# Inverse roots of all normalisations as one power on GpSimd, in a two-sequence encoder layer

## The chip, the cores and the metric

One NeuronCore of a Trainium2 chip. The core's engines are TensorE (PE; its weight loads are the rows "PEld"), VectorE (DVE), ScalarE (ACT), GpSimd (POOL), and SyncE (SP), which issues most DMAs. Each engine runs its own instructions in order and waits for the others through semaphores. The metric is the device time of one launch in microseconds; it covers both sequences and all weights.

## The reference

One encoder layer, run on two independent sequences of 512 tokens (`x_prompt`, `x_sample`), all in float32, with D = 1024 and a feed-forward width of 2816:

```python
def rms_norm(x, g):
    y = x * lax.rsqrt(jnp.mean(x * x, axis=-1, keepdims=True) + EPS)      # EPS = 1e-6
    return y * g

def encoder_layer(x, ...):
    x = x + 0.5 * swiglu(rms_norm(x, ffn1_norm), ffn1_w_gate, ffn1_w_up, ffn1_w_down)
    h = rms_norm(x, mix_norm)
    proj = h @ w_in                                  # 13 parts: aq ak av mq mk mv gates o g_att g_mlstm
    aq = apply_rope(rms_norm(aq, q_norm), cos, sin)  # 8 heads of 64, a root for each token and head
    ak = apply_rope(rms_norm(ak, k_norm), cos, sin)  # 2 heads of 64
    att = gqa_block_attention(aq, ak, av)
    mem = mlstm_bidirectional(mq, mk, mv, ...)       # 4 heads of 128, each head normalised by its rms
    merged = sigmoid(g_att) * (att @ w_up_att) + sigmoid(g_mlstm) * (mem @ w_up_mlstm)
    x = x + merged @ w_out
    x = x + 0.5 * swiglu(rms_norm(x, ffn2_norm), ffn2_w_gate, ffn2_w_up, ffn2_w_down)
    return x                                         # then rms_norm(x, final_norm)
```

Each `rms_norm` needs one number for each token (or token and head): 1/sqrt(mean of squares + EPS). How that number is made is what the change is about.

## The kernel before

**Layout and stages.** The residual stream of a sequence is kept transposed (`xs[s]`: channels on partitions, 8 blocks of 128, tokens along the row). For both sequences in turn there is a first feed-forward block, the mixing block (projections, attention, the mLSTM memory, merging, output projection), and a second feed-forward block; most products are made of high and low parts of the operands (`split`, `put`), each product several matmuls of 128x512. The weights of the first pass are split once, parked in DRAM and read again for the second sequence (`load_w`). Times in the profile by stage: first feed-forward of both sequences to about 655 us; mixing of the first sequence (s=0) to about 1015; mixing of the second (s=1) to about 1440; second feed-forward of both to 2060; final norm to the end.

**Order.** The program is written once, in Python, and a scheduler orders each engine's instructions by priority, which follows the order of writing; `with shifted(n)` moves what stands inside it later by n steps (or earlier, for n below 0). A shift is counted in written instructions, so an edit that removes some of them also moves others. On the chip each engine then keeps its order strictly: a matmul that waits for a small result holds up every matmul behind it.

**From squares to the root.** `sq_add` makes squares on ScalarE (L152, L155) and adds them on GpSimd (L156). `col_sums` turns the sums with TensorE (L203) into a PSUM bank and sums the rows on VectorE (L205): one column of sums for each block of 128 tokens, so 128x4 for a sequence. `rstd_cols` (L162) scales by 1/n and adds EPS, and `rsqrt_cols` makes the root on VectorE: a shift and a subtraction on the integer bits as first guess (L171, L173), then three Newton steps of three instructions each:

```python
        for _ in range(3):
            t = t_()
            V.scalar_tensor_tensor(t, y, -0.5, y, op0=ALU.mult, op1=ALU.mult)
            V.tensor_tensor(t, t, a, op=ALU.mult)
            r = t_()
            V.scalar_tensor_tensor(r, t, 1.5, y, op0=ALU.add, op1=ALU.mult)
            y = r
```

(L189, L190, L192.) With the scaling that is twelve instructions; without it, eleven. For a width of two the steps are written column by column (L177, L182, L184), fifteen instructions. `bcast_psum` turns the four columns with TensorE so that each token's root stands in every partition (L213), and `bcast_cols` copies that to SBUF (L219).

**Where roots are made.** There are 21 of them:

- two at the start, from token rows (`rows_rstd`, 128x4, sums L1258);
- one for each sequence ahead of the mixing block (`stats`, 128x4), near 655 and 760 us;
- one for the keys (`kv_done`, 128x8) and one for the queries (`q_done`, 128x32) of each sequence, near 674 and 697 us and near 1019 and 1041 us; their sums come from `sumsq` (L785). `rope_apply` multiplies by the root (L796) and rotates; `q_rope` turns the rotated queries with TensorE (L941);
- four for the memory's heads of each sequence (128x4), from 861 to 948 and from 1250 to 1331 us; the broadcast is written 160 steps later (`shifted(160)`);
- one for each sequence ahead of the second feed-forward block (128x4), near 1154 and 1441 us;
- one for the final norm of the first sequence (`finish0`, 128x4), near 2062 us, and two for the second (`finish1`, two columns each, for the token blocks 0, 1 and 2, 3).

**The last microseconds.** `finish1_upper` turns and squares the upper channels of the second sequence; `finish1(th)` turns the lower ones (L1411), squares them in two parts (`square`, L1437), adds the sums (L1457, L1460), makes the root, and `put_out` multiplies (L1418 on VectorE, L1420 on ScalarE, L1422 on VectorE) and stores (L1423). L606 is VectorE's eviction of the last down projection, which adds the residual.

GpSimd does little besides the additions L156: copies of gates (L868), a gate of the memory's output, a table (L699), and the issue of a few small DMAs (the gains of the norms, among others).

Of the kernel before, what the change touches and what calls it, by code (L numbers as in the profile page):

```python
# [8 lines left out]
F32 = mybir.dt.float32  # L9
F32R = mybir.dt.float32r  # L10
I32 = mybir.dt.int32
AF = mybir.ActivationFunctionType
ALU = mybir.AluOpType
# [3 lines left out]
P = 128  # L17
S = 512
D = 1024
# [3 lines left out]
EPS = 1e-6  # L23
# [3 lines left out]
def encoder(ctx, tc, I, outs):  # L27
    nc = tc.nc
    cpool = ctx.enter_context(tc.tile_pool(name="cpool", bufs=1))
# [4 lines left out]
    spool = ctx.enter_context(tc.tile_pool(name="spool", bufs=4))  # L34
# [7 lines left out]
    def nm(s):  # L42
        n_id[0] += 1
        return f"{s}_{n_id[0]}"
# [71 lines left out]
    def PT():  # L116
        return pt.tile([P, S], F32, tag="t", name=nm("pst"))
# [9 lines left out]
    make_identity(nc, ident)  # L127
    ones = cpool.tile([P, P], F32, name="ones")
    nc.vector.memset(ones, 1.0)
    pw = PT()[:, 0:P]  # L130
    warm = cpool.tile([P, 1], F32, name="warm")
    nc.scalar.activation(warm, ones[:, 0:1], AF.Silu)
# [16 lines left out]
    def sq_add(src, acc, tag="t2", qtag="f2", eng=None):  # L149
        if acc is None:  # L150
            acc = T2(F32, tag)
            nc.scalar.activation(acc, src, AF.Square)  # L152
            return acc
        q = T2(F32, qtag)
        nc.scalar.activation(q, src, AF.Square)  # L155
        (eng or nc.gpsimd).tensor_tensor(acc, acc, q, op=ALU.add)  # L156
        return acc

    def rstd_cols(v, width, n):

        a = spool.tile([P, width], F32, tag=f"rs{width}", bufs=5 if width > 2 else 10, name=nm("rs"))
        nc.vector.tensor_scalar(a, v, 1.0 / n, EPS, op0=ALU.mult, op1=ALU.add)  # L162
        return rsqrt_cols(a, width)

    def rsqrt_cols(a, width):

        def t_(dt=F32):
            return spool.tile([P, width], dt, tag=f"rs{width}", bufs=5 if width > 2 else 10, name=nm("rs"))
        V = nc.vector
        b = t_(I32)  # L170
        V.tensor_scalar(b, a.bitcast(I32), 1, None, op0=ALU.logical_shift_right)  # L171
        y_ = t_(I32)
        V.tensor_scalar(y_, b, -1.0, 1597463007.0, op0=ALU.mult, op1=ALU.add)  # L173
        y = y_.bitcast(F32)
        if width <= 2:
            h = spool.tile([P, width], F32, tag=f"rsh{width}", bufs=2, name=nm("rsh"))
            V.tensor_scalar(h, a, -0.5, None, op0=ALU.mult)  # L177
            cols = [slice(i, i + 1) for i in range(width)]
            for _ in range(3):
                t, r = t_(), t_()  # L180
                for c in cols:
                    V.scalar_tensor_tensor(t[:, c], y[:, c], h[:, c], y[:, c], op0=ALU.mult, op1=ALU.mult)  # L182
                for c in cols:
                    V.scalar_tensor_tensor(r[:, c], t[:, c], 1.5, y[:, c], op0=ALU.add, op1=ALU.mult)  # L184
                y = r
            return y
        for _ in range(3):
            t = t_()
            V.scalar_tensor_tensor(t, y, -0.5, y, op0=ALU.mult, op1=ALU.mult)  # L189
            V.tensor_tensor(t, t, a, op=ALU.mult)  # L190
            r = t_()
            V.scalar_tensor_tensor(r, t, 1.5, y, op0=ALU.add, op1=ALU.mult)  # L192
            y = r
        return y

    def stats(acc):

        return rstd_cols(col_sums(acc), 4, D)

    def col_sums(acc, bs=(0, 1, 2, 3)):  # L200
        p = PT()
# [558 lines left out]
    def mix(s, xh, xl, early=None, extra=None, after=None):  # L760
# [20 lines left out]

        def sumsq(t, to):
            q2 = T2()
            nc.scalar.activation(q2, t, AF.Square)
            V_.tensor_reduce(to, q2.rearrange("p (h e) -> p h e", e=DA), axis=AX.X, op=ALU.add)  # L785

        def rope_apply(t, rq, tab, bsel):
# [25 lines left out]
        def kv_done(pk):  # L813
            for b in range(4):
                nc.scalar.activation(kraw3[:, b, :], pk[b][:, 0:P], AF.Copy, scale=r[s][:, b:b + 1])
                nc.scalar.activation(Gt[:, b * 16:(b + 1) * 16], pk[b][:, 2 * P:2 * P + 16], AF.Copy,
                                     scale=r[s][:, b:b + 1])
                pv = pk[b][:, P:2 * P].rearrange("p (k e) -> p k e", k=HK)
                nc.scalar.activation(Vst[:, b, :, 0:DA], pv, AF.Copy, scale=r[s][:, b:b + 1])
                V_.scalar_tensor_tensor(Vst[:, b, :, DA:2 * DA], pv, r[s][:, b:b + 1], f(Vst[:, b, :, 0:DA]),  # L820
                                        op0=ALU.mult, op1=ALU.subtract)
            ssk = small(8, "ssk")
            sumsq(kraw, ssk)
            ko = rope_apply(kraw, rstd_cols(ssk, 8, DA), tabs[1], None)
            ko3 = ko.rearrange("p (g e) -> p g e", e=DA)
            nc.scalar.activation(kst[:, :, 0, 0, :], ko3, AF.Copy)
            nc.scalar.activation(kst[:, :, 0, 1, :], ko3, AF.Copy)
            V_.tensor_tensor(kst[:, :, 1, 0, :], ko3, f(kst[:, :, 0, 0, :]), op=ALU.subtract)
            V_.tensor_tensor(kst[:, :, 1, 1, :], ko3, f(kst[:, :, 0, 1, :]), op=ALU.subtract)
# [3 lines left out]
        def q_done(pq):  # L833
            ssq = small(32, "ssq")
            for b in range(4):
                t = T2()
                nc.scalar.activation(t, pq[b], AF.Copy, scale=r[s][:, b:b + 1])
                sumsq(t, ssq[:, b * 8:(b + 1) * 8])
                qraw.append(t)
            rq.append(rstd_cols(ssq, 32, DA))  # L840

        def k_turn():
            for hk in range(HK):
# [306 lines left out]
        def mem_out(h, Ts):  # L1150
            vm = Vm[0]
            po = PO()
            hs_ = slice(h * P, (h + 1) * P)
            turned = []
            for j in range(4 + 1):
                if j < 4:
                    p = PT()
                    for i in range(4):
                        nc.tensor.transpose(p[:, i * P:(i + 1) * P], Ts[i][0][:, j * P:(j + 1) * P], ident)
                    ph, pl = T2(F32R), T2(F32R)  # L1160
                    split(p, ph, pl)
                    turned.append((j, ph, pl))
                if j >= 1:
                    t, ph, pl = turned.pop(0)
                    with shifted(15):
                        for n, (a, b) in enumerate(((0, ph), (1, ph), (0, pl))):
                            nc.tensor.matmul(po, vm[:, a, t, hs_], b, start=(t == 0 and n == 0),  # L1167
                                             stop=(t == 3 and n == 2))
            h2 = T2()
            nc.scalar.activation(h2, po, AF.Square)  # L1170
            og = ogs[h]
            V_.tensor_tensor(og, og, po, op=ALU.mult)
            rh = rstd_cols(col_sums(h2), 4, DM)
            with shifted(160):
                Rh = bcast_psum(rh)
                V_.tensor_tensor(og, og, Rh, op=ALU.mult)
                split(og, mem[:, h, 0, :], mem[:, h, 1, :])
# [70 lines left out]
    def rows_rstd(s, engines):  # L1248

        sq = [spool.tile([P, 4], F32, tag="cs4", bufs=4, name=nm("cs4")) for _ in range(2)]  # L1250
        for b in range(4):
            for i in range(2):
                x_, to = raws[s][:, b, i * S:(i + 1) * S], sq[i][:, b:b + 1]
                if engines[i] is V_:
                    V_.scalar_tensor_tensor(orow[3 + i], x_, 1.0, x_, op0=ALU.mult, op1=ALU.mult, accum_out=to)
                else:
                    nc.scalar.activation(orow[3 + i], x_, AF.Square, accum_out=to)
        V_.tensor_tensor(sq[0], sq[0], sq[1], op=ALU.add)  # L1258
        return rstd_cols(sq[0], 4, D)

    def scaled(to, x_, k, R_):
        V_.scalar_tensor_tensor(to, x_, g1[:, k:k + 1], R_, op0=ALU.mult, op1=ALU.mult)
# [184 lines left out]
    def finish1(th):  # L1447
        bs = slice(2 * th, 2 * th + 2)
        cut = 2 * P
        ps_ = PS(), PT()  # L1450
        for ks in (0, 1), (2, 3):
            for i in range(2):
                turn_out(1, 2 * th + i, 0, ps_[i], ks)
                if ks[0] == 0:
                    square(1, 2 * th + i, ps_[i][:, 0:cut])
        sm, a = small(2, "fs2"), small(2, "fs2")
        V_.scalar_tensor_tensor(sm, sq1[:, 0, bs], EPS, sq1[:, 1, bs], op0=ALU.add, op1=ALU.add)  # L1457
        for i in range(2):
            square(2, 2 * th + i, ps_[i][:, cut:S])
        V_.tensor_tensor(a, sm, sq1[:, 2, bs], op=ALU.add)  # L1460
        r = rsqrt_cols(a, 2)
        with shifted(0 if th else LATER):
            for j in range(4):
                i, half = j % 2, 1 - j // 2
                b = 2 * th + i
                put_out(1, b, half, upper[b] if half else ps_[i], r[:, i:i + 1])
# [55 lines left out]
```

## Time and profile before

| | us |
|---|---|
| median of 3 runs | 2086.05 (2085.86 to 2088.21) |
| the profiled execution | 2088.21 |
| its span in the profile | 2088.2 |
| TensorE busy | 2063.1 (99%), 9488 matmuls |
| VectorE busy | 1573.0 (75%), 2870 instructions |
| ScalarE busy | 894.6 (43%), 1645 instructions |
| GpSimd busy | 100.3 (5%), 106 instructions |

Busy time counts from a record's start to its end, and matmuls are pipelined, so a busy TensorE need not be one at its peak. The granted TensorE clock is at nine tenths or more of full speed in all 40 slices of the span. In rows of the timeline the first number is the start in us from the beginning of the span, the second the length in us; then engine, line, operation, output<-inputs with shape, and a count; a bracket at the end gives the engine's idle time before it and what ended it. In rows of groups (by line) stand busy time in us, the mean of one in ns, and the idle time just before them. "L171" is line 171 of the kernel.

### The profile page before, as it was taken

What the parts mean: (1) busy time and instruction counts of PE and PEld (TensorE: products, weight loads), DVE (VectorE), ACT (ScalarE), POOL (GpSimd) and SP (SyncE); (2) the same over time, 40 slices, a digit from 0 to 9 for tenths busy, and PEclk for the clock granted to TensorE, in tenths of its full rate; (3) what the DMA queues carried; (4) which work ended last, traced back from release to release, by engine and by line L of the source; (5) the groups of instructions that cost most, each with busy time, mean ns of one, the idle gap of its engine ahead of it and who ended that gap; (6) DMA issues with size and microseconds to landing.
All of it is one profiled execution on the core that took longest, in us unless ns stands there. A gap on an engine that the chain in (4) does not pass through costs nothing.

```text
span 2088.2 us, 27312 instructions
## 1 busy us (share of the span) xinstructions
PE 2063.1 (99%) x9488; PEld 1694.4 (81%) x9488; DVE 1573.0 (75%) x2870; ACT 894.6 (43%) x1645; POOL 100.3 (5%) x106
## 2 busy tenths in 40 slices
PE   8999999999999999999999999999999999999998
PEld 6888888888888877888877788888888888888887
DVE  6888888786797899575557945545888888785797
ACT  6544444443234566463344543324444444442222
POOL 1000000001003012000110000001000000000010
PEclk9999999999999999999999999999999999999999
DMA  8656555699766655777675345677656555599753
GB/s 274 203 174 197 192 171 182 204 343 358 260 225 245 213 170 198 259 234 272 204 273 191 121 152 185 206 247 248 203 170 213 186 177 182 182 350 343 272 189 115
DMA packets 304186, 458.53 MB, mean 220 GB/s; under 512 B 20304, under 2 KB 170848, under 8 KB 303024
## 3 DMA queue, kind: packets, MB, share of 16 engines
q1 hardware_dynamic: 303456, 455.52, 64.9%
q0 software_dynamic: 592, 1.27, 0.3%
q8 instruction: 75, 1.23, 0.2%
q14 instruction: 63, 0.52, 0.1%
HBM read 289.82 MB, written 166.89 MB: 219 GB/s over the span
## 4 chain that ended last, share of the span: by engine, by line
PE 90%; DVE 4%; DMA 3%; ACT 1%; issue 1%; SPq 0%; DVEq 0%; POOL 0%; ACTq 0%; POOLq 0%
PE mm L755 18%; PE pss L333 17%; PE pst L333 11%; PE mm L333 9%; PE mm L589 9%; PE pst L589 4%; PE pss L589 4%; PE mm L739 4%; PE pso L589 3%; PE pso L739 1%; PE pso L1028 1%; PE pso L1167 1%; PE pss L1001 1%; PE pst L755 1%; PE pss L755 1%; PE pss L1117 1%
## 5 line engine op out<-in xcount | busy, mean ns | idle before, releaser
L755 PE MATMUL mm<-xh,w 128*128 128x512 f32 x896 | 292.2, 396 | 2.0 <-DMA w<-wpark 2.0
L333 PE MATMUL pss<-xc,w 128*128 128x512 f32 x1056 | 256.2, 391 | 1.0 <-DVE t L364 1.0
L333 PE MATMUL mm<-xc,w 128*128 128x512 f32 x1056 | 253.6, 391 | 3.3 <-ACT w L291 1.0
L333 PE MATMUL pst<-xc,w 128*128 128x512 f32 x1056 | 253.6, 389 | 0.0
L333 PEld LDWEIGHTS pss<-xc,w 128*128 128x128 f32 x1056 | 196.8, 188 | 48.3 <-DVE t L364 7.9
L333 PEld LDWEIGHTS mm<-xc,w 128*128 128x128 f32 x1056 | 197.2, 188 | 46.7 <-ACT w L291 2.0
L333 PEld LDWEIGHTS pst<-xc,w 128*128 128x128 f32 x1056 | 198.2, 188 | 41.2
L755 PEld LDWEIGHTS mm<-xh,w 128*128 128x128 f32 x896 | 168.0, 189 | 36.4 <-DVE f L1204 1.9
L589 PE MATMUL mm<-rt,w 128*128 128x512 f32 (+1 forms) x819 | 188.4, 384 | 0.0
L755 PE MATMUL mm<-xl,w 128*128 128x512 f32 x448 | 176.4, 394 | 0.0
L589 PEld LDWEIGHTS mm<-rt,w 128*128 128x128 f32 x819 | 151.3, 188 | 29.8
L291 ACT ACTIVATE w<-t 128x512 fp32r<-128x512 f32 x176 | 107.1, 627 | 141.1 <-issue 55.2
L292 DVE TENSOR_TENSOR w<-t,w 128x512 fp32r<-128x512 f32 x176 | 118.2, 687 | 51.8 <-ACT w L291 49.7
L333 PE MATMUL pss<-xc,f 128*128 128x512 f32 x528 | 126.8, 389 | 0.0
L333 PEld LDWEIGHTS pss<-xc,f 128*128 128x128 f32 x528 | 99.1, 188 | 20.6
L657 ACT ACTIVATE w<-wr 128x512 fp32r<-128x512 f32 x72 | 45.2, 632 | 138.1 <-PE pso L589 65.7
L755 PEld LDWEIGHTS mm<-xl,w 128*128 128x128 f32 x448 | 84.7, 189 | 17.0
L657 ACT ACTIVATE w<-t 128x512 fp32r<-128x512 f32 x82 | 51.8, 632 | 107.4 <-PE pst L589 62.4
L589 PE MATMUL pss<-rt,w 128*128 128x512 f32 x396 | 93.7, 389 | 0.0
L589 PE MATMUL pst<-rt,w 128*128 128x512 f32 x396 | 93.7, 389 | 0.0
L240 DVE TENSOR_TENSOR w<-wr,w 128x1024 fp32r<-128x1024 f32 (+1 forms) x56 | 69.6, 1243 | 23.6 <-ACT w L239 22.9
L589 PEld LDWEIGHTS pst<-rt,w 128*128 128x128 f32 x396 | 74.3, 188 | 15.4
(336 smaller groups left out, 3656.4 us busy)
## 6 DMA issues: line engine op xcount, KB each, us to landing
rt<-rbuf SPq DMA_DIRECT2D x154, 512.0 KB, 5.4
wpark<-w SPq DMA_DIRECT2D x104, 512.0 KB, 3.5
w<-wpark SPq DMA_DIRECT2D x104, 512.0 KB, 4.6
wr<-in_ffn_w_gate_dram SPq DMA_DIRECT2D x62, 512.0 KB, 5.2
rbuf<-tab SPq DMA_DIRECT2D x102, 256.0 KB, 4.0
wr<-in_ffn_w_up_dram SPq DMA_DIRECT2D x44, 512.0 KB, 4.6
rbuf<-f SPq DMA_DIRECT2D x72, 256.0 KB, 4.0
wr<-in_w_in_dram SPq DMA_DIRECT2D x36, 512.0 KB, 5.7
```

The lines of the kernel that those rows point to most:

```text
L240: pin(lo_eng.tensor_tensor(lo, raw, f(hi), op=ALU.subtract))
L291: pin(nc.scalar.activation(t[:, 0], src, AF.Copy))
L292: pin(V_.tensor_tensor(t[:, 1], src, f(t[:, 0]), op=ALU.subtract))
L333: nc.tensor.matmul(p, a[:, k, :], xt[:, b, k, :], start=(first and k == 0 and i == 0), stop=(k == HK_ - 1 and i == 2), skip_group_check=True)
L589: nc.tensor.matmul(p, u[:, a, d * P:(d + 1) * P], r[:, b, ts], start=(first and q == 0 and k == 0), stop=(q == len(us) - 1 and k == 2), sk ...
L657: nc.scalar.activation(hi, src, AF.Copy)
L739: nc.tensor.matmul(p[b][:, :N], a[:, k, bs], w_[:, kl, :], start=(k == 0 and i == 0), stop=(k == KD - 1 and i == 2))
L755: nc.tensor.matmul(p, a[:, k, :], b, start=(k == 0 and i == 0), stop=(k == n - 1 and i == 2))
L1001: nc.tensor.matmul(p, qT[:, h, b * P:(b + 1) * P], kv[:, hk * 2 + j, :], start=(j == 0), stop=(j == 1))
L1028: nc.tensor.matmul(po, Vst[:, kv_, hk, :], w, start=(kv_ == 0 and i == 0), stop=(kv_ == 3 and i == 1))
L1117: nc.tensor.matmul(p, qk[a][:, isl], qk[b], start=(n == 0), stop=(n == 2))
L1167: nc.tensor.matmul(po, vm[:, a, t, hs_], b, start=(t == 0 and n == 0), stop=(t == 3 and n == 2))
```

## The change

`rsqrt_cols` is gone. `rstd_cols` now takes sums of squares that carry 1/n already, adds EPS with one instruction of GpSimd (left out where the sums hold EPS already), and raises to the power -0.5 with a second one, whose exponents come from a constant tile `nhalf`. The squares get the factor n^-0.5 on ScalarE (`scale=`), where the kernel squares with ScalarE; at the start, where VectorE squares half of the rows, the factor 1/n stands in that instruction, and EPS is added where the two halves are summed. In all 21 powers and 17 additions of GpSimd take the place of 248 instructions of VectorE; the tiles of the small columns get 4 buffers instead of 5 or 10. What reads the roots, and how they are broadcast, is as before. The scheduler orders the whole program anew.

```diff
@@
+    nhalf = cpool.tile([P, 32], F32, name="nhalf")
+    nc.gpsimd.memset(nhalf, -0.5)
...
@@ sq_add
-            nc.scalar.activation(acc, src, AF.Square)
+            nc.scalar.activation(acc, src, AF.Square, scale=D ** -0.5)
...
-        nc.scalar.activation(q, src, AF.Square)
+        nc.scalar.activation(q, src, AF.Square, scale=D ** -0.5)
...
-    def rstd_cols(v, width, n):
-
-        a = spool.tile([P, width], F32, tag=f"rs{width}", bufs=5 if width > 2 else 10, name=nm("rs"))
-        nc.vector.tensor_scalar(a, v, 1.0 / n, EPS, op0=ALU.mult, op1=ALU.add)
-        return rsqrt_cols(a, width)
-
-    def rsqrt_cols(a, width):
...
+    def rstd_cols(v, width, eps=EPS):
+
+        a = spool.tile([P, width], F32, tag=f"rs{width}", bufs=4, name=nm("rs"))
+        if eps:
+            nc.gpsimd.tensor_scalar(a, v, eps, None, op0=ALU.add)
+            v = a
+        nc.gpsimd.tensor_tensor(a, v, nhalf[:, 0:width], op=ALU.pow)
+        return a
 
     def stats(acc):
 
-        return rstd_cols(col_sums(acc), 4, D)
+        return rstd_cols(col_sums(acc), 4)
...
@@ sumsq
-            nc.scalar.activation(q2, t, AF.Square)
+            nc.scalar.activation(q2, t, AF.Square, scale=DA ** -0.5)
...
@@ kv_done
-            ko = rope_apply(kraw, rstd_cols(ssk, 8, DA), tabs[1], None)
+            ko = rope_apply(kraw, rstd_cols(ssk, 8), tabs[1], None)
...
@@ q_done
-            rq.append(rstd_cols(ssq, 32, DA))
+            rq.append(rstd_cols(ssq, 32))
...
@@ mem_out
-            nc.scalar.activation(h2, po, AF.Square)
+            nc.scalar.activation(h2, po, AF.Square, scale=DM ** -0.5)
...
-            rh = rstd_cols(col_sums(h2), 4, DM)
+            rh = rstd_cols(col_sums(h2), 4)
...
@@ rows_rstd
-                    V_.scalar_tensor_tensor(orow[3 + i], x_, 1.0, x_, op0=ALU.mult, op1=ALU.mult, accum_out=to)
+                    V_.scalar_tensor_tensor(orow[3 + i], x_, 1.0 / D, x_, op0=ALU.mult, op1=ALU.mult, accum_out=to)
                 else:
-                    nc.scalar.activation(orow[3 + i], x_, AF.Square, accum_out=to)
-        V_.tensor_tensor(sq[0], sq[0], sq[1], op=ALU.add)
-        return rstd_cols(sq[0], 4, D)
+                    nc.scalar.activation(orow[3 + i], x_, AF.Square, scale=D ** -0.5, accum_out=to)
+        V_.scalar_tensor_tensor(sq[0], sq[0], EPS, sq[1], op0=ALU.add, op1=ALU.add)
+        return rstd_cols(sq[0], 4, 0)
...
@@ finish1
-        r = rsqrt_cols(a, 2)
+        r = rstd_cols(a, 2, 0)
```

More of the change, by code (lines that the diff above doesn't have):

```diff
@@ L165, in rsqrt_cols @@
-    def rsqrt_cols(a, width):
[L167 to L194, printed above, removed]
```

## The prediction

> **What bounds the kernel now.** I read the page first (busy shares), then the timeline at each place where an inverse root stands. From the page:
>
> ```profile
> span 2088.2 us, 27312 instructions
> ## 1 busy us (share of the span) xinstructions
> PE 2063.1 (99%) x9488; PEld 1694.4 (81%) x9488; DVE 1573.0 (75%) x2870; ACT 894.6 (43%) x1645; POOL 100.3 (5%) x106
> ```
>
> TensorE is the bound: 2063.1 of 2088.2 us. No saving elsewhere can reach the time except through its 25.1 us of idle time, and much of that lies at the two ends, before the first inputs have landed and after the last matmul. The change frees VectorE, which is busy for 75%. So the question is narrow: at which of the 21 inverse roots does TensorE wait, or the end depend, on the small VectorE instructions, and what stands there afterwards.
>
> **The prices.** GpSimd (POOL) executes no power now. Its nearest rows, by shape, and a handover from VectorE:
>
> ```profile
> L156 POOL TENSOR_TENSOR R<-R,f 128x512 f32<-128x512 f32 x17 | 24.8, 1460 | 156.1 <-ACT f L155 142.8 <-ACT R L152 12.7
> ...
> L699 POOL TENSOR_TENSOR tab<-f,gb 128x128 f32<-128x128 f32 x4 | 2.0, 521 | 0.0
> ```
>
> ```profile
> 672.17 0.23 DVE L862 TENSOR_TENSOR gt<-gt,gbias 128x64 f32<-128x64 f32 x1
> ...
> 672.46 0.20 POOL L868 COPY Fs<-gt 128x16 f32<-128x16 f32 x1 [1.41 <-DVE gt L862]
> ```
>
> A two-input pass costs (1460-521)/384 = 2.45 ns a column and 521-128x2.45 = 207 ns beside it. The eps addition on 4 columns is then 0.22 us. A handover costs 672.46-672.40 = 0.06, and I take the same for one out of POOL and between two of its own. With X for the power: from sums to root 0.06+0.22+0.06+X+0.06 = 0.4+X with the addition, 0.1+X without.
>
> X is the unknown. From below: one pass, 0.21 us for 4 columns and 0.28 for 32. From above, by rows: POOL does what the twelve VectorE instructions did, each at the price of a pass of its own, 12x0.21 = 2.5 us for 4 columns and 12x0.28 = 3.4 for 32. I take 0.2 us + 50 ns a column, an estimate: one dispatch, and in each column some twenty passes' worth of arithmetic, about twice the chain's operations, since a general power must handle any exponent. X is then 0.3 (2 columns), 0.4 (4), 1.8 (32): near the lower end, because the fixed price is paid once and not twelve times.
>
> **The end of the kernel: gain 1.75 us.** ScalarE there, and the last sums on VectorE:
>
> ```profile
> 2078.43 0.72 ACT L1420 ACTIVATE t<-t,rs 128x512 f32<-128x512 f32 x1
> 2079.04 0.38 ACT L1437 ACTIVATE f<-pss 128x256 f32<-128x256 f32 x1
> ...
> 2081.87 1.33 ACT L1420 ACTIVATE t<-t,rs 128x512 f32<-128x512 f32 x2 [2.00 <-DVE rs L184]
> ```
>
> ```profile
> 2079.91 0.16 DVE L1460 TENSOR_TENSOR fs<-fs,sq 128x2 f32<-128x2 f32 x1
> ```
>
> The last root is on the path: its sums are done at 2080.07, ScalarE starts on it at 2081.87, and the stores follow. These 1.80 us become 0.1+X = 0.4: 1.4 less. The first half's root moves too: in the new order its L1420 (at 2078.43 now) goes ahead of ScalarE's squares, so the square L1437 no longer queues behind it from 2078.43 to 2079.04. It can start when TensorE has turned its input; of the 0.61 us I take 0.35, and the last sums come that much earlier. Together 2.05-X = 1.75. The change adds a wait here: in VectorE's queue two evictions (L606), which TensorE's last transposes need, now stand behind an instruction that waits for the first root. That bites only where the power takes longer than the chain it replaces, some 2.4 us.
>
> **The query norms of the first sequence (128x32): loss 0.75 us.**
>
> ```profile
> 696.48 0.66 DVE L785 TENSOR_REDUCE ssq<-t 128x8 f32<-128x512 f32 x1
> ...
> 700.33 0.69 DVE L796 TENSOR_TENSOR t<-t,rs 128x512 f32<-128x512 f32 x1
> ...
> 704.30 1.04 PE L941 MATMUL pst<-ident,t 128*128 128x128 f32 x8
> ```
>
> The new program's order puts the first turning of rotated queries (L941) 1.8 us earlier, counted in the matmuls ahead of it: TensorE, strictly in order, arrives at 702.5. Its input takes 704.30-700.33, about 4.0 us, from the start of L796, which needs the root. The sums are done at 696.48+0.66 = 697.14 and the root at 697.55+X, so the turning can start at 701.55+X, and TensorE waits X-1.05 = 0.75. The same norm of the second sequence is done long before VectorE gets to its first use and costs nothing.
>
> **Broadcasts (L213) that come earlier in TensorE's order: loss 2.45 us before relief.** The column sums (L203, then VectorE's L205) at three of them:
>
> ```profile
> 756.75 0.63 PE L203 MATMUL pst<-ident,R 128*128 128x128 f32 x4
> ...
> 758.35 0.68 DVE L205 TENSOR_REDUCE cs<-pst 128x4 f32<-128x512 f32 x1
> ```
>
> ```profile
> 1150.66 0.60 PE L203 MATMUL pst<-ident,R 128*128 128x128 f32 x4
> ...
> 1151.65 0.68 DVE L205 TENSOR_REDUCE cs<-pst 128x4 f32<-128x512 f32 x1
> ```
>
> ```profile
> 1440.31 0.69 DVE L205 TENSOR_REDUCE cs<-pst 128x4 f32<-128x512 f32 x1 [0.75 <-PE pst L203]
> ...
> 1443.45 0.65 PE L213 MATMUL pst<-ident,rs 128*128 128x128 f32 x4 [0.18 <-DVE rs L192]
> ```
>
> Near 757 the broadcast followed L203 after 10.7 us of matmuls; in the new order after 2.5, and L203 itself stands 1.1 earlier: due at 756.75-1.1+2.5 = 758.15. Its sums are done at 759.03, the root at 759.43+X = 759.8: a wait of 1.65. Near 1151 the 10.3 us have become 1.8, due at 1152.46; sums 1152.33, root 1152.73+X = 1153.1: a wait of 0.65. Near 1441 it is due 1.8 earlier than the 1443.27 at which TensorE arrives now, 1441.47; root 1441.0+0.4+X = 1441.8: a wait of 0.35 against 0.18, loss 0.15. Of the other column roots the nearest to its use is a head's:
>
> ```profile
> 925.64 0.68 DVE L205 TENSOR_REDUCE cs<-pst 128x4 f32<-128x512 f32 x1
> ...
> 934.40 0.62 PE L213 MATMUL pst<-ident,rs 128*128 128x128 f32 x4
> ```
>
> It is due 6.2 us earlier, at 928.2, and stands at 926.32+0.4+X = 927.1, in time up to X = 1.5.
>
> **What is freed: gain 0.9.** In the first sequence's attention VectorE is nearly as full as TensorE (columns: length, then PE, PEld, DVE, ACT, POOL):
>
> ```profile
> 700.00:725.00 25.00, 25.00 (x130) 20.65 (x129) 24.30 (x50) 14.93 (x31) 0.00 (x0) 1.00 0.53 176
> 750.00:775.00 25.00, 24.16 (x124) 19.38 (x123) 23.72 (x54) 14.56 (x30) 4.69 (x4) 1.00 0.60 189
> 800.00:830.00 30.00, 29.16 (x140) 22.88 (x139) 25.50 (x58) 20.31 (x45) 6.70 (x4) 1.00 0.55 187
> ```
>
> In the second and the third row TensorE idles 0.84 us each beside a busy VectorE, some 1.8 us with the crumbs between. The query norms' chain and that of the 757 root leave VectorE there. I take half of the 1.8. Bounds: nothing; or all of it, and the 1.65 us wait too, if VectorE gets to the sums as soon as L203 allows.
>
> **The start: nothing.**
>
> ```profile
> 10.88 0.16 DVE L1258 TENSOR_TENSOR cs<-cs,cs 128x4 f32<-128x4 f32 x1
> ...
> 14.41 0.72 PEld L213 LDWEIGHTS pst<-ident,rs 128*128 128x128 f32 x4 [0.47 <-ACT t L1243]
> ...
> 36.04 1.06 ACT L291 ACTIVATE w<-wr 128x1024 fp32r<-128x1024 f32 x1 [1.05 <-DMA wr<-in_ffn_w_gate_dram]
> ```
>
> The first broadcast waits for a ScalarE copy (L1243) that frees its bank, 3.4 us after the sums: that covers the root until X passes 3.2. Four small gain loads on POOL's queue now stand behind the first two roots and go out near 30 us; nobody reads them before the first down projection ends. In SP's order one weight load moves ahead of a store: up to 1.05 gained at ScalarE's wait at 36.04, or lost, if the gain loads now collide with it. I take 0. Squares with a scale cost what squares without did, and the scaled sum replaces a plain one: nothing.
>
> **Sum.** -1.75 +0.75 +1.65 +0.65 +0.15 -0.9 = +0.55 us. With c the price of a column in us, X = 0.2+c x columns, it is -1.7+46c; 32 of the 46 are the query norms. The profiled execution took 2088.21 us with its span of 2088.2; the median of the three runs is 2.16 below. On the median: 2086.6 us.
>
> One more thing can lengthen POOL's instructions, its port:
>
> ```profile
> 659.32 9.00 POOL L156 TENSOR_TENSOR R<-R,f 128x512 f32<-128x512 f32 x5 [12.74 <-ACT R L152]
> ```
>
> Five additions took 9.00 where five times the mean is 7.3: 0.34 us more each, at a stretch where VectorE evicts at the same time. With two POOL instructions at each of four places that decide, it is up to 2.7 us; I take none and keep it for the range.
>
> The Trainium skill (SBUF — State Buffer, Who interferes with whom) makes this a rule against the change: VectorE and GpSimd share a port pair that is held for a whole instruction, and an instruction of VectorE with two SBUF operands blocks one of GpSimd that reads SBUF. By that rule the longer additions above are waits for VectorE and not work, and the powers inherit them; the trace agrees as far as additions that differ in length at one shape can show it.
>
> **Rivals.** *The power is slow,* and TensorE's order, written for a quick one, waits for POOL. At the upper end by rows (2.5 and 3.4 us): end +0.45, query norms +2.35, 757 +2.9, 1151 +2.8, 1441 +2.25 = +10.75, 2096.8 us. It turns the sum past +4.2 us from c = 0.128, a power of 4.3 us on 32 columns; c = 0.3 gives 2098.1. For it: no row shows POOL evaluating anything beyond one addition or product. Against it: POOL's price per instruction is only 0.2 us, and most of its price per column would have to be new.
>
> *VectorE was the brake.* Its relief then ends the idle time in attention (1.8 us), the sums come at once, the early broadcasts cost nothing (and the 0.18 goes), and the weight load gains: -1.85 (end, cheapest X) -1.8 -0.2 -1.05 = -4.9, 2081.15 us. For it: 24.30 of 25 us busy. Against it: TensorE is at 25.00 of 25 in the same row, so VectorE's lateness is covered there already.
>
> That the change doesn't do what it says has no room: the new order of POOL holds 21 powers and 17 additions, and VectorE's chains are gone.
>
> **Chances.** 0.2% is 4.2 us, about what a measurement of this kernel can tell from no change. Sum near zero: 0.58. Slow power: 0.32, of which prices beyond c = 0.37 hold 0.12. VectorE's relief: 0.10. These are the chances of same, slower and faster. The range goes from 2080.5, past the relief case, to 2101 (c = 0.37). The likeliest case alone: 2083.2 (cheapest X, all relief in attention, the weight load's gain) to 2090.2.
>
> **What would show it.** Right: the last L1420 starts about 0.4 us after the last sums; powers near 0.4 us on 4 columns and 1.8 on 32; TensorE waits about 1.6 and 0.6 us at the 757 and 1151 broadcasts; its busy time is unchanged. Wrong: powers above 2 us on 4 columns or a wait of several us at L941 near 702 (slow power); or hardly any idle TensorE from 700 to 830 (VectorE).

## The result, and the profile after

| | median us | against the kernel before |
|---|---|---|
| kernel before | 2086.22 (7 runs, 2085.29 to 2088.21) | |
| changed kernel | 2092.48 (7 runs, 2090.92 to 2095.36) | 1.0031, 95% interval 1.0022 to 1.0041 |

The change makes the kernel 6.3 us slower. That lies in the forecast's range, but only because the range was drawn out for a rival: it is not the likeliest case (2086.6), it is the prediction's first rival, the slow power. The page of the changed kernel (span; busy time by engine):

```profile
span 2089.2 us, 27103 instructions
...
PE 2062.1 (99%) x9488; PEld 1696.6 (81%) x9488; DVE 1537.8 (74%) x2612; ACT 896.4 (43%) x1645; POOL 137.8 (7%) x145
```

VectorE is busy for 35 us less, with 258 instructions fewer (not the 248 given with the change), GpSimd for 37.5 us more, and TensorE about as long as before: most of what was saved was saved where nobody waited. The spans alone would show 1.0 us. The profiled execution was the fastest of the seven here, 2090.92 us, 1.8 above its span. In every other run the time lies 1.7 to 1.9 us above the span. If that holds for the first trace of before, its 2088.2 stands for about 2090.0, an unlucky execution, and not for the 2088.21 that the prediction set beside it.

The price, from the groups of instructions by line and shape on GpSimd (busy, mean ns, idle time before):

```profile
L167 POOL TENSOR_TENSOR rs<-rs,nhalf 128x4 f32<-128x4 f32 x13 | 13.5, 1039 | 1.1
L167 POOL TENSOR_TENSOR rs<-rs,nhalf 128x32 f32<-128x32 f32 x2 | 10.9, 5460 | 0.2
...
L165 POOL TENSOR_SCALAR rs<-cs 128x4 f32<-128x4 f32 x13 | 3.9, 297 | 281.0 <-DVE cs L179 225.1 <-DVE asm L981 55.9
L167 POOL TENSOR_TENSOR rs<-rs,nhalf 128x8 f32<-128x8 f32 x2 | 3.3, 1669 | 0.2
...
L167 POOL TENSOR_TENSOR rs<-fs,nhalf 128x2 f32<-128x2 f32 x2 | 1.4, 696 | 15.9 <-DVE fs L1434 15.9
...
L165 POOL TENSOR_SCALAR rs<-ssq 128x32 f32<-128x32 f32 x2 | 0.6, 307 | 41.9 <-DVE ssq L759 41.9
```

A power costs (5460-1039)/28 = 158 ns a column and 0.41 us beside it: 0.70, 1.04, 1.67 and 5.46 us on 2, 4, 8 and 32 columns. VectorE's chain took 1.85 us on 2 columns and, where nothing came between, 2.35 on 4 and 2.63 on 32. So the power wins 1 us on 2 columns and, with its addition, 1 on 4, and loses 3 on 32.

The place where it loses, the query norms of the first sequence (timeline):

```profile
695.28 0.31 POOL L165 TENSOR_SCALAR rs<-ssq 128x32 f32<-128x32 f32 x1 [21.22 <-DVE ssq L759]
695.67 5.46 POOL L167 TENSOR_TENSOR rs<-rs,nhalf 128x32 f32<-128x32 f32 x1
...
701.16 0.69 DVE L770 TENSOR_TENSOR t<-t,rs 128x512 f32<-128x512 f32 x1 [5.37 <-POOL rs L167]
...
705.06 1.94 PE L915 MATMUL pst<-ident,t 128*128 128x128 f32 x8 [4.38 <-DVE t L632]
```

TensorE stands for 4.38 us at the first turning of rotated queries (L915, the old L941), VectorE for 5.37 us ahead of it. Then there is a second loss, in the stretches (length, busy PE, PEld, DVE, ACT, POOL, then TensorE's granted clock):

```profile
695.00:700.00 5.00, 4.99 (x31) 4.08 (x29) 0.79 (x2) 2.28 (x4) 4.64 (x2) 1.00 0.32 77
...
705.00:707.00 2.00, 1.94 (x9) 1.97 (x10) 2.00 (x5) 0.60 (x1) 0.00 (x0) 0.50 0.00 0
707.00:709.00 2.00, 2.00 (x6) 1.52 (x6) 1.41 (x3) 1.97 (x4) 0.00 (x0) 0.50 0.00 0
709.00:711.00 2.00, 2.00 (x9) 1.59 (x8) 1.88 (x4) 1.66 (x4) 0.00 (x0) 0.78 0.55 217
711.00:713.00 2.00, 2.00 (x12) 1.67 (x11) 2.00 (x4) 0.00 (x0) 0.00 (x0) 1.00 1.01 399
```

After the wait TensorE's granted clock is 0.50 for about five microseconds and its matmuls of 128x512 start 0.43 us apart instead of 0.23. Counted from the matmul near 700 us to the one of the same number near 718, the changed kernel takes 6.6 us longer: 4.4 of waiting, 2.2 of slow work (to some 0.3 us, since the order of the matmuls differs there). The Trainium skill (TensorE: Matmul & The Clock Gate, What's actually happening) says that the clock halves after an idle window of about 3.4 us and comes back after a busy one of that length. By that rule a wait of 4.4 us costs half of the 3.4 us on top, 1.7 as an estimate of mine; the trace shows 2.2. The half clock lasts 6.83 us there, twice that length: it begins at 703.04, 2.4 us into the wait, and holds for 4.8 us after it.

The broadcasts that TensorE reaches too early (L177 turns the sums, L187 is the broadcast):

```profile
759.61 0.60 PE L177 MATMUL pst<-ident,R 128*128 128x128 f32 x4
...
761.26 0.69 DVE L179 TENSOR_REDUCE cs<-pst 128x4 f32<-128x512 f32 x1
...
762.35 1.04 POOL L167 TENSOR_TENSOR rs<-rs,nhalf 128x4 f32<-128x4 f32 x1
...
763.44 0.65 PE L187 MATMUL pst<-ident,rs 128*128 128x128 f32 x4 [0.90 <-POOL rs L167]
...
1154.83 0.65 PE L187 MATMUL pst<-ident,rs 128*128 128x128 f32 x4 [0.96 <-POOL rs L167]
...
1443.94 0.65 PE L187 MATMUL pst<-ident,rs 128*128 128x128 f32 x4 [1.07 <-POOL rs L167]
```

All three now wait for the power, about 1 us each. In the first trace of before these waits were 0, 0 and 0.18 us.

The final norms, first sequence and then the last root:

```profile
2064.46 1.04 POOL L167 TENSOR_TENSOR rs<-rs,nhalf 128x4 f32<-128x4 f32 x1
...
2065.53 0.75 DVE L1396 SCALAR_TENSOR_TENSOR t<-pss,rs,t 128x512 f32<-128x512 f32 x1 [1.48 <-POOL rs L167]
...
2066.34 0.33 PE L1385 MATMUL pss<-ident,xs 128*128 128x128 f32 x1 [0.70 <-DVE t L1396]
...
2078.73 0.48 DVE L1392 TENSOR_SCALAR t<-t,rs 128x512 f32<-128x512 f32 x1 [0.81 <-POOL rs L167]
2079.14 0.42 DVE L580 SCALAR_TENSOR_TENSOR xs<-mm,xs 128x256 f32<-128x256 f32 x1
...
2080.13 0.41 DVE L580 SCALAR_TENSOR_TENSOR xs<-pso,xs 128x256 f32<-128x256 f32 x1
...
2081.89 0.16 DVE L1434 TENSOR_TENSOR fs<-fs,sq 128x2 f32<-128x2 f32 x1 [0.63 <-ACT f L1411]
2082.14 0.70 POOL L167 TENSOR_TENSOR rs<-fs,nhalf 128x2 f32<-128x2 f32 x1 [3.44 <-DVE fs L1434]
2082.87 1.33 ACT L1394 ACTIVATE t<-t,rs 128x512 f32<-128x512 f32 x2 [1.01 <-POOL rs L167]
```

At the end the change does what it should: the sums are done at 2082.05 and ScalarE starts at 2082.87, after 0.82 us instead of 1.80.

### The profile page after: what moved, and what is told of

The parts are those of the page before. It is cut to its first block, busy times and chain, and to the rows that moved or that the text cites. A ratio compares the mean times of both kernels' runs of the same rounds, so it can differ in the third digit from the quotient of the medians.

```text
span 2089.2 us, 27103 instructions
## 1 busy us (share of the span) xinstructions
PE 2062.1 (99%) x9488; PEld 1696.6 (81%) x9488; DVE 1537.8 (74%) x2612; ACT 896.4 (43%) x1645; POOL 137.8 (7%) x145
## 4 chain that ended last, share of the span: by engine, by line
PE 93%; DVE 2%; DMA 1%; ACT 1%; issue 1%; POOL 1%; SPq 0%; DVEq 0%; POOLq 0%; ACTq 0%
PE mm L729 18%; PE pss L307 17%; PE pst L307 11%; PE mm L307 11%; PE mm L563 8%; PE pst L563 4%; PE pss L563 4%; PE mm L713 4%; PE pso L563 3%; PE pso L1002 1%; PE pso L713 1%; PE pss L975 1%; PE pst L994 1%; PE pso L1141 1%; PE pss L729 1%; PE pst L729 1%
## 5 line engine op out<-in xcount | busy, mean ns | idle before, releaser
L213 ACT ACTIVATE w<-wr 128x1024 fp32r<-128x1024 f32 (+1 forms) x56 | 57.4, 1028 | 76.0 <-PE mm L729 28.2
```

The costliest lines, as they stand in the source:

```text
L213: pin(nc.scalar.activation(hi, raw, AF.Copy))
```

## The experiments

Theory: the loss is the power's price on 32 columns, at the one place where TensorE waits for it. First rival of these experiments: it is spread over the broadcasts that come early and the final norms. Second rival: it is the new order of TensorE, or transfers that fall differently from run to run. Differences below are to the median of the kernel before on the same chip, since chips differ by up to 2 us in that median.

| kernel | median us | difference | ratio, 95% interval |
|---|---|---|---|
| after_again | 2092.55 | +7.1 | 1.0035 (1.0023 to 1.0048) |
| q_chain | 2087.77 | +2.3 | 1.0013 (1.0004 to 1.0022) |
| q_power | 2091.61 | +6.1 | 1.0028 (1.0017 to 1.0039) |
| q_quarters | 2086.70 | +1.2 | 1.0005 (0.9996 to 1.0013) |
| q_later | 2090.67 | +4.7 | 1.0024 (1.0015 to 1.0033) |
| q_twice | 2097.29 | +11.3 | 1.0058 (1.0044 to 1.0072) |
| end_power | 2086.08 | +0.1 | 1.0000 (0.9991 to 1.0009) |
| bc_late | 2083.50 | -2.7 | 0.9993 (0.9984 to 1.0002) |
| bc_only | 2090.69 | +6.5 | 1.0030 (1.0019 to 1.0040) |
| best | 2083.69 | -2.5 | 0.9989 (0.9980 to 0.9998) |

**Two second traces.** No edit in either.

> The changed kernel once more, for a second trace and a ratio on the same chip as the next three. Theory (price at the query norms): 6 us above the kernel before (2092.5 against 2086.2 so far), with TensorE waiting about 4.4 us at the first turning of rotated queries near 705 us and its matmuls at half pace for some 4 us after it, as in the first trace. Rival (the loss is spread over many small waits or comes from transfers that fall differently from run to run): the wait at 705 stays, but the balance of the rest of the trace moves by several us between the two traces, in the start and near 1096 us.

> The kernel before once more, for a second trace. The first showed TensorE waiting 2.0 us for parked weights near 1096 us and its matmuls at half pace after it (3.5 us together), and 0.5 us near 1490; the traces of the changed kernel and its variants show nearly none of it, at whatever time they come there. If this is chance of the one execution, the second trace lacks it or has another size; if it belongs to the kernel before, it is there again with 2.0 us. At the places of the broadcasts (757, 1151, 1441 us) it should show the waits of the first: 0, 0 and 0.18 us.

The loss is there again, with a wait of 4.39 us. The traces are laid side by side by the number of the matmul. The table gives how much longer each stretch took than in the first trace of before:

| stretch (us, by the first trace of before) | changed kernel, two traces | before, second trace | end_power (before but for its end) |
|---|---|---|---|
| start to 700 | -1.95, +0.36 | +0.10 | -1.69 |
| 700 to 718, query norms | +6.57, +6.52 | 0.0 | 0.0 |
| 718 to 1090, attention, 757 broadcast | -0.14, +0.18 | +1.92 | +1.10 |
| 1090 to 1151 | -3.49, -4.00 | -3.15 | -3.43 |
| 1151 to 1435, 1151 broadcast | +0.45, +0.50 | -0.64 | -0.58 |
| 1435 to 1480, 1441 broadcast | +0.85, +0.88 | 0.0 | 0.0 |
| 1480 to 2051 | -1.19, -1.29 | -1.22 | +0.29 |
| 2051 to 2076, first sequence's norm | +0.82, +0.85 | 0.0 | 0.0 |
| 2076 to the end | -1.01, -1.05 | 0.0 | -0.71 |

The start moves by two microseconds with each execution, and 1090 to 1151 was chance of the first trace of before. There TensorE waited twice for weights that came back from DRAM:

```profile
1096.64 0.47 PE L755 MATMUL mm<-xh,w 128*128 128x512 f32 x1 [1.55 <-DMA w<-wpark]
...
1097.80 1.18 PE L755 MATMUL mm<-xh,w 128*128 128x512 f32 x2 [0.46 <-DMA w<-wpark]
```

and in its second trace once:

```profile
1098.24 0.73 PE L755 MATMUL mm<-xh,w 128*128 128x512 f32 x2 [0.47 <-DMA w<-wpark]
```

So a single pair of traces misleads here: the first pair would have credited the change with 3.5 us that it did not earn. What repeats is +6.5, then about 1 lost at 1151, 0.86 at 1441, 0.8 at 2062, and about 1 gained at the end. In the stretch from 718 to 1090, the waits at the 757 broadcast included, about 1 is gained against the mean of the three traces with the old chains there, but those three differ by up to 1.9 us among themselves, so its size is uncertain.

**The old chain, or the power, for the query norms alone.** `rstd_vec` is the old chain on sums that carry 1/n, `rstd_pow` the power with 1/n in its first instruction:

```diff
 # q_chain, from the changed kernel
-            rq.append(rstd_cols(ssq, 32))
+            rq.append(rstd_vec(ssq, 32))
 # q_power, from the kernel before
-            rq.append(rstd_cols(ssq, 32, DA))
+            rq.append(rstd_pow(ssq, 32, DA))
```

> The changed kernel, with only the two query norms (128x32) made by VectorE's old chain again. Theory: the wait of 4.4 us and the slow matmuls behind it (2.4 us more) go, 6.6 us less than the changed kernel: 2085.9, the same as the kernel before. Rival (spread: broadcasts that come early near 757, 1151 and 1441 us and the two ends): only some 1 to 2 us less, 2090.5 to 2091.5. Rival (it is the new order of TensorE, not the power): no change, 2092.5.

> The kernel before, with only the two query norms made by one power of GpSimd each (and one instruction for 1/n and EPS ahead of it). Theory: the whole loss appears, 6 to 7 us above the kernel before: 2092.5 to 2093. Rival (spread): 1 to 2 us above, 2087 to 2088.

q_power alone brings 6.1 us, the theory's number; in its trace TensorE waits 4.32 us at the turning. q_chain gives back 4.8 of the 7.1 us, where 6.6 was expected. In its trace TensorE does not wait at the turning, now L952:

```profile
698.10 0.69 DVE L807 TENSOR_TENSOR t<-t,rv 128x512 f32<-128x512 f32 x1
...
702.06 1.04 PE L952 MATMUL pst<-ident,t 128*128 128x128 f32 x8
```

The order of TensorE depends on the root's engine too: with the chain the turning goes back behind 1.8 us of matmuls. For the 2.3 us that remain there are the broadcasts (waits of 0.86, 0.93 and 1.06 us in its trace) and the first sequence's norm, which q_chain keeps. Both rivals fall as the main cause; the first holds for that rest.

**Quarters.** Each block of 128 tokens gets its own power (the small tiles of eight columns get 6 buffers instead of 4):

```diff
-            rq.append(rstd_cols(ssq, 32))
+            for b in range(4):
+                rq.append(rstd_cols(ssq[:, b * 8:(b + 1) * 8], 8))
...
-            qo = rope_apply(qraw[b], rq[0][:, b * 8:(b + 1) * 8], ...
+            qo = rope_apply(qraw[b], rq[b], ...
```

> The changed kernel, with each query norm's 128x32 power cut into four of 128x8, each with its own EPS addition; a block of 128 tokens waits only for its own. A power on 8 columns took 1.67 us and its addition 0.25, against 5.46 and 0.31 on 32. Theory: the first root is there 3.85 us earlier, TensorE waits 0.5 us instead of 4.4 and keeps its pace; 6 us less than the changed kernel, 2086.5. Rival (spread): 1 to 2 us less, 2090.5 to 2091.5. If what counts is the sum over all 32 columns (7.7 us in four pieces), it is slower than the changed kernel by up to 2 us.

```profile
695.90 1.67 POOL L167 TENSOR_TENSOR rs<-rs,nhalf 128x8 f32<-128x8 f32 x1
...
699.73 1.25 POOL L165 TENSOR_SCALAR rs<-ssq 128x8 f32<-128x8 f32 x1
...
701.06 2.06 POOL L167 TENSOR_TENSOR rs<-rs,nhalf 128x8 f32<-128x8 f32 x1
...
705.03 1.04 PE L916 MATMUL pst<-ident,t 128*128 128x128 f32 x8
```

5.9 us come back with all roots still powers, and L916 starts with no wait. What counts is when the first 8 columns are there, not the sum over 32. The third addition took 1.25 us where another one took 0.24, and its power 2.06 instead of 1.67, while VectorE was rotating. This fits the port of the prediction: the rule of the Trainium skill weighed there (SBUF — State Buffer, Who interferes with whom) bears on powers as well, with 1.0 us for that addition and 0.4 for its power here. In the changed kernel VectorE stood still beside the long power, and the 13 powers on 128x4 took 1.04 us each; one addition on 128x4, at 949.11 us, took 1.13 us instead of 0.23, and TensorE shows no wait for it.

**Only the order.** The shift of the turnings, for the first sequence:

```diff
-                with shifted(60):
+                with shifted(130 if s == 0 else 60):
                     p = PT()
```

> The changed kernel, with the turnings of the first sequence's rotated queries written 130 steps later instead of 60: TensorE does 5.4 us more of its other matmuls first. Same power, same price. Theory (the price counts only because the order puts TensorE there too early): the 4.4 us wait and the slow matmuls behind it go, about 6 us less than the changed kernel: 2086.5; up to 2 us above that if the attention's first scores now come late. Rival (the chain root, rotation, scores is the limit): the wait moves to the scores behind it, and the time stays at 2092.

Only about 2.4 us came back (7.1 against 4.7), not 6. The first L915 no longer waits, but a matmul behind it does:

```profile
704.17 0.73 ACT L631 ACTIVATE t<-t 128x256 fp32r<-128x256 f32 x2 [5.22 <-DVE t L781]
...
708.95 0.54 PE L729 MATMUL mm<-xh,w 128*128 128x512 f32 x1 [2.13 <-ACT w L213]
```

VectorE stands for 5.4 us ahead of its first use of the root, and ScalarE for 5.2 us behind VectorE. The split of the next weights (L213) is queued behind that on both engines. So neither my theory (order alone would do) nor the rival (the scores wait) held: the wait moved to the weights, and behind its 2.13 us the clock was halved again, for 3.41 us.

**A second power.** It uses the sums without EPS:

```diff
+            G_.tensor_tensor(rd, ssq, nhalf[:, 0:32], op=ALU.pow)
```

> The changed kernel, with a second power on 128x32 behind the first for each query norm (it takes the sums without EPS, and its result is the one used): 5.5 us more on GpSimd ahead of the first rotated query. Theory: TensorE's wait grows from 4.4 to 9.9 us, and the slow matmuls behind it cost the same 2.4 us, since they follow any wait of that kind: 5.5 us above the changed kernel, 2098. If the slow stretch grows with the wait, 2099 to 2101. Rival (the loss is elsewhere): no change.

```profile
710.82 1.94 PE L917 MATMUL pst<-ident,t 128*128 128x128 f32 x8 [9.89 <-DVE t L632]
```

The wait grew by 5.5 us, as expected, and the place by 4.7 (11.25 against 6.55): the slow work cost 0.8 us less this time, 1.4 instead of 2.2, and the half clock ended 3.1 us after the wait instead of 4.8. So it does not grow with the wait.

**The last roots alone.**

```diff
-        r = rsqrt_cols(a, 2)
+        r = spool.tile([P, 2], F32, tag="rp2", bufs=4, name=nm("rp"))
+        nc.gpsimd.tensor_tensor(r, a, nhalf[:, 0:2], op=ALU.pow)
```

> The kernel before, with only the last two roots (128x2) made by a power of GpSimd, 0.70 us each in the traces. By the prediction's step with this price 1.35 us less than the kernel before, 2084.5. By the trace of the changed kernel 1.0 us less: the last root shortens the path by 1.26 us, from TensorE's last matmul to the end, but two evictions of VectorE wait behind instructions that need the first root, and TensorE's last transposes come 0.25 us later. Rival (the evictions cost more): nothing gained, 2085.9. In the trace TensorE should show about 0.4 and 0.1 us of idle time ahead of its last transposes, and ScalarE start on the last root 0.8 us after the sums.

By the time this is undecided: +0.1 us with an interval of about 1.9 to either side. By the trace the end is 0.71 us shorter, where 1.0 to 1.35 was expected; a transpose there waits 0.35 us for an eviction that stands behind a product with the first root.

**The broadcasts later.**

```diff
-    m0 = mix(0, *nhl[0], None, lambda: mid_stats(1), prep1)
+    m0 = mix(0, *nhl[0], None, lambda: mid_stats(1, 0, 160), prep1)
...
         r[s] = stats(acc2[s])
-        R2[s] = bcast_cols(r[s])
+        with shifted((180, 40)[s]):
+            R2[s] = bcast_cols(r[s])
```

> The changed kernel, with the three broadcasts near 757, 1151 and 1441 us written later (160, 180 and 40 steps), so that TensorE does 6.4, 7.5 and 5.7 us of other matmuls between the column sums and the broadcast, instead of 2.7, 2.0 and 1.6. Theory (TensorE waits there because the new order leaves a root of 1.3 us with its handovers too little room): the waits of 0.9, 0.95 and 1.06 us in the traces of the changed kernel go, and their sum of 2.9 us: 2089.6 against 2092.5, with the 4.4 us wait near 705 as it was. Rival (other work, freed by the root, ends up waiting for the later broadcast): nothing gained, 2092.5.

The kernel that ran as bc_late had the quarters of the query norms as well, which this expectation leaves out. It is to be compared with q_quarters, which ran on another chip, so by the differences: the theory's number is 1.2-2.9 = -1.7 us, measured -2.7, one more than expected and within the two intervals. The power is long done when TensorE comes to the third broadcast, here the root near 1436 us:

```profile
1436.18 1.04 POOL L167 TENSOR_TENSOR rs<-rs,nhalf 128x4 f32<-128x4 f32 x1
...
1440.15 0.27 PE L187 MATMUL pst<-ident,rs 128*128 128x128 f32 x1
```

> The changed kernel, with only the three broadcasts written later and each query norm one power on 128x32 as before. (The run bc_late, whose expectation spoke of this, also had the query norms in quarters.) Theory, terms add: 2.9 us less than the changed kernel, 2089.6, with the 4.4 us wait near 705 us and the slow matmuls behind it as they were; against bc_late the query norms' 6.1 to 6.7 us. Rival (the later broadcasts did most of it and the query norms' wait is made up elsewhere): 2083.5 to 2085.

Without the quarters the same shifts show no gain: +6.5 us, where 2.9 less than the changed kernel's +6.3 or +7.1 was expected, so the terms do not add. The waits at 1151 and 1441 are gone (0.8 us less at each), but the one at 757 came back elsewhere in attention, with TensorE waiting for ScalarE behind VectorE:

```profile
778.92 1.60 DVE L982 TENSOR_SCALAR t<-t,asm 128x512 f32<-128x512 f32 x1
778.94 1.30 POOL L941 TENSOR_TENSOR box<-box,tab 128x512 f32<-128x512 f32 x1 [0.66 <-DMA box<-ebuf]
...
785.27 0.50 PE L1002 MATMUL pso<-t,kv 128*128 128x512 f32 x1 [2.40 <-ACT t L631]
```

L941 is an addition that GpSimd had before too (L967, 16 of 128x512, 23.9 us in all), which the account of GpSimd's work ahead of the prediction leaves out. L982 mostly takes 0.48 us; beside this addition it took 1.60. That this collision made the 2.40 us wait is argued from these rows and not tried.

**All together.** Quarters, late broadcasts, and:

```diff
-                with shifted(LATER):
+                with shifted(LATER - 10):
                     finish0()
...
-        r = rstd_cols(a, 2, 0)
+        r = rstd_cols(a, 2, 0) if th else rsqrt_cols(a, 2)
```

> All that the runs point to, on the changed kernel: the query norms' power in four of 128x8; the three broadcasts later as in the run beside this one; the final norm of the first sequence written 10 steps earlier, so that its column sums stand among TensorE's last matmuls again; and the first of the last two roots on VectorE's old chain, so that no eviction waits for it, the second as a power. From the changed kernel: 6.7 (query norms) + 2.9 (broadcasts) + 0.8 (first sequence's final norm) + 0.2 (evictions) less, 2081.9; that is 4 us below the kernel before, of which 1.0 is the last root, and up to 2 us that VectorE is relieved of in attention. Rival (the freed time of VectorE is covered by TensorE anyway): only the last root's 1.0 us stays, 2085.

2.5 us below the kernel before, and faster by 0.02 to 0.20% of its time: a gain, of which little more than the sign is shown. The sum of the terms promised 2081.9, and on the same chip bc_late came to the same time without the last two edits. By the trace the earlier norm brings its stretch back to the kernel before (+0.05 us), but the end is no shorter than in the changed kernel (-0.95). In TensorE's stretch from 750 to 830 us the sum row of the kernel before (its second trace) and of this one:

```profile
sum 80.00, PE 76.58 PEld 60.34 DVE 74.74 ACT 48.08 POOL 15.53; mean PE 76.58 PEld 60.34 DVE 74.74 ACT 48.08 POOL 15.53
```

```profile
sum 80.00, PE 79.07 PEld 62.45 DVE 71.02 ACT 49.89 POOL 16.66; mean PE 79.07 PEld 62.45 DVE 71.02 ACT 49.89 POOL 16.66
```

TensorE idles 0.9 us there instead of 3.4. The two other traces with the old chains idle 1.9 (the first of before) and 3.3 us (end_power), so the difference is 1 to 2.5. It has the sign of VectorE's relief, the prediction's second rival; how much of it the later broadcasts made is not separated.

## Why the prediction was right or wrong

| term | at 50 ns a column | at the measured price | by the traces |
|---|---|---|---|
| end | -1.75 | 2.05-0.70: -1.35 | -1.0 |
| query norms | +0.75 | 5.46-1.05: +4.4 | +6.5 |
| 757 | +1.65 | +2.3 | +0.9 (wait) |
| 1151 | +0.65 | +1.3 | +0.9 |
| 1441 | +0.15 | +0.8 | +0.86 |
| relief | -0.9 | -0.9 | -1.9 (what is left of 718 to 1090) |
| first sequence's norm | 0 | 0 | +0.8 |
| sum | +0.55 | +6.55 | +7.1 (measured +6.3, +7.1) |

The sum at the measured price, 6.55, comes near the measured 6.3 and 7.1 partly by luck: the query norms were 2.1 us dearer than their term and the first sequence's norm 0.8, the 757 broadcast 1.4 and the relief about 1 cheaper. Of the two signs named for a slow power, the wait of several us at the first turning is there (4.38); powers above 2 us on 4 columns are not (1.04).

**The step that failed is the power's price:** "near the lower end", 50 ns a column, measured 158. The argument was that the fixed price is paid once; that held (0.41 us, where 0.2 was taken), but the price per column is sixty times that of an addition's pass, 158 against 2.45 ns, and not twenty. On 32 columns that puts it above the end "by rows" too, 5.46 against 3.4, so this end was no bound. On 4 columns, where 1.04 lies between 0.21 and 2.5, the rows did bound it. The rival had its decision point at 128 ns and this is past it; its chance of 0.32 was too low for a price for which no row spoke.

**Query norms.** The wait was worked out rightly: X-1.05 = 4.41 us, measured 4.38, though the times given there make it X-0.95, so the last tenth is luck. It left out what the wait does to TensorE afterwards, 2.2 us of half pace.

**757.** Too high by 1.4. I let TensorE turn the sums 1.1 us earlier but kept VectorE's sums at their old time; in the trace they follow L177 at the old distance, so both moved. The rest is the matmuls between, 2.9 us instead of 2.5. At 1441 the same working was right to a tenth.

**The end.** The wait in VectorE's queue, named there, was said to bite only where the power takes longer than the chain. It bites with a power of 0.70. In the kernel before the last eviction ran between two steps of the chain, where this row stands:

```profile
2077.63 0.15 DVE L184 SCALAR_TENSOR_TENSOR rs<-rs,rs 128x1 f32<-128x1 f32 x1
2077.70 0.41 DVE L606 SCALAR_TENSOR_TENSOR xs<-pso,xs 128x256 f32<-128x256 f32 x1
```

An engine that waits can't do this, and the evictions at 2079.14 and 2080.13 came behind L1392 and L1396. TensorE's last transposes stood 0.25 us later. That the evictions made it is argued: with the first root back on VectorE (best) a transpose waits 0.71 us for ScalarE instead, and the 0.2 us did not come back.

**The first sequence's norm** was counted among the roots that are in time. The root itself is quicker (1.5 us from the sums to its first use, 3.0 before), but the new order turns the sums 2.1 us of matmuls later, and TensorE waits 0.70 us for a bank instead of 0.28. That is half of the 0.8; the other half comes between 2066 and 2076 us without a wait of TensorE above 0.1, and its cause is open. In best, where the norm is written 10 steps earlier, the whole stretch is back to +0.05 us.

**Right:** TensorE's busy time did not change, the start moved only by chance, the second sequence's query norms cost nothing that the traces show, and the port, which lengthened one addition, made no wait of TensorE that shows.

## What to carry to other kernels

Price an operation that no row shows by what it does in each column, and give the unknown slope, not the fixed part, the wide range: one power was cheap on 4 columns and the whole loss on 32. Where a wide small operation stands ahead of blocks that are used one after another, cut it so that the first block waits only for its own part. When work leaves a busy engine for an idle one, the first engine now stands still at the use, and everything queued behind it in order stands too; moving one reader later moved that wait and gave back 2.4 of 7.1 us.

## What the hardware showed that I had not expected

A wait of TensorE can cost more than its length: one of 4.4 us brought 2.2 us of slow work at half clock, one of 9.9 us brought 1.4. In the first trace of before (first pair of rows) two waits of 1.55 and 0.46 us, 2.0 in all, were enough, in q_later (second pair) a single one of 2.13; in bc_only (third pair) one of 2.40 was not (stretches; the second number is TensorE's busy time, the granted clock is the third from the end):

```profile
1094.46:1097.87 3.41, 1.40 (x6) 0.55 (x4) 1.39 (x2) 0.63 (x1) 0.00 (x0) 1.00 0.93 329
1097.87:1101.29 3.42, 3.42 (x8) 2.70 (x9) 0.00 (x0) 0.00 (x0) 0.00 (x0) 0.50 1.01 351
...
705.86:709.27 3.41, 1.28 (x8) 0.87 (x7) 3.06 (x7) 1.95 (x4) 0.00 (x0) 1.00 0.00 0
709.27:712.69 3.42, 3.42 (x10) 2.40 (x9) 3.42 (x6) 2.26 (x4) 0.00 (x0) 0.50 0.88 350
...
781.33:784.74 3.41, 1.54 (x7) 0.94 (x5) 3.38 (x7) 2.15 (x6) 1.29 (x1) 1.00 0.34 136
784.74:788.15 3.41, 2.88 (x16) 2.34 (x17) 3.41 (x7) 1.25 (x3) 0.00 (x0) 1.00 0.48 154
```

In all 13 traces the stretches of half clock ahead of the last microseconds are 3.41, 6.83 or 10.24 us long, and the full-clock stretches between them are whole multiples of 3.41 as well. Count the time between 45 and 2060 us in such steps from the changes of the clock. Behind each step at full clock with at most 1.4 us of busy TensorE the clock went to half (seven cases), and behind none with 1.5 us or more. So where a wait falls among the steps matters beside its length: 4.32 us in q_power cost one step of half clock, 4.38 us in the changed kernel two. After the single waits of 0.9 to 1.1 us at the broadcasts the clock stayed at 1.00. The idle window of 3.4 us of the Trainium skill (TensorE: Matmul & The Clock Gate, What's actually happening) thus need not be idle throughout: 1.4 us of matmuls stood in the first row shown.
